# After the last U block, V blocks load into U's buffers, and the last LN weights and rows come later, from GpSimd's queue

## The chip, the cores and the metric

One core of a Trainium2 chip runs the whole program. The metric is the device time of one execution in microseconds, the median of several. Engines are named as in the profile: PE is TensorE, DVE VectorE, ACT ScalarE, POOL GpSimd, SP the engine that here only issues DMAs.

## The reference, cut to what matters

One layer of an encoder on 512 prompt frames and 32 sample frames of width 1024: a token mixer, a layer norm, then PEER (16384 single-neuron experts, 8 heads, the best 16 each) and a second layer norm. The change lies in PEER and the second norm:

```python
    t1, i1 = lax.top_k(s1, PEER_TOPK)
    t2, i2 = lax.top_k(s2, PEER_TOPK)
    ...
    g = jax.nn.softmax(top, axis=-1)
    u = jnp.take(u_tab, idx, axis=0)
    act = jax.nn.gelu(jnp.einsum("nhkd,nd->nhk", u, xb).astype(jnp.float32))
    vv = jnp.take(v_tab, idx, axis=0)
    return jnp.einsum("nhk,nhkd->nd", (g * act).astype(xb.dtype), vv)
...
    y = layer_norm(DN_ALPHA * h + peer_ffn(h, peer_w_query, peer_keys_1, peer_keys_2, peer_u, peer_v), ln2_g, ln2_b)
```

## The kernel before

The expert stage takes the last 1,000 us or so. 384 of the 544 tokens are done densely: all 16384 experts are computed for them in 128 blocks of 128 experts. Block b of the U table gives the activations `acts` (`up`), later these are multiplied with a matrix of gates that is zero where an expert was not chosen, and block b of the V table is multiplied with them and added up in six PSUM banks (`down`). The other tokens, the sample frames (`S`) and the last 128 prompt frames (`P3`), are done by gathers: an indirect DMA of GpSimd fetches one chosen row of U or V for each of 128 partitions into a tile `gat`, and VectorE makes a dot product of it (L1100) or adds it to `acc` (L1115).

Matmuls of 32-bit numbers are made of three products: every operand is split into a high part (a cast on ScalarE) and a low part (a subtraction on VectorE). For a block of V that is `vr`, the raw tile that SP loads, `vh` (L1184) and `vl` (L1185); for the gated activations `pwh` (L1217) and `pwl` (L1218). A block of V is 18 matmuls of 512 columns.

The loop of `experts` runs over `it`. In each step it computes U block `it`, and V block b = it - 27 (AHEAD is 27). From it = 128 on only V blocks are left, 101 to 127, of which the last four stand behind the loop. Each V block also loads `gt`, a piece of the gate matrix, into one of three buffers (L1204), multiplied into `acts` at L1211. A few gathers follow in each step; each waits for the load of that step's block (`pace`).

The tiles of one tag share a ring of buffers: 6 of tag `u` (raw, high and low part of U blocks), 8 of tag `v` (the same of V blocks), 6 of `gat` (gathered rows, the raw tiles of the last four V blocks, the scratch of the second layer norm), two of `pwh` and `pwl`. An instruction that fills a buffer waits for all who used it before. At it = 128 `ln_loads` puts the two weight rows `lnw` of the second layer norm into `u` buffers, at it = 132 `rows_back` puts the three 128-row tiles `hback` there that hold the dense tokens' residual. Both are issued from ScalarE's queue.

The order of each engine's instructions is not that of the code: a scheduler sorts them when the program is built. An engine then executes its own strictly in order, and a DMA that has to wait for its buffer holds up all that stands behind it on the same queue.

Of the kernel before, what the change touches and what calls it, by code (L numbers as in the profile page):

```python
# [32 lines left out]
P = 128  # L33
# [12 lines left out]
NK = 128  # L46
# [41 lines left out]
AHEAD = 27  # L88
# [5 lines left out]
NV = 8  # L94
GATHER = AHEAD
RATE = (1, 1), (28, 10), (31, 10), (12, 10)
BACK = 4
ROUTE = (5, 2), (1, 1)


class Build:
# [1044 lines left out]
    def experts(self, es):  # L1146
        tc, nc, A = self.tc, self.nc, self.A
# [28 lines left out]
        acts, ups, vload, gg = self.acts, {}, {}, {}  # L1176

        def table(ap, name, stage=None):
            tile_ = dict(gat=lambda dt, n: pool.tile([P, D], dt, tag="gat", name=n, bufs=NGAT), u=lambda dt, n: pool.tile([P, D], dt, tag="u", name=n, bufs=NU),
                         v=lambda dt, n: self.vtile(dt, [P, D], n))  # L1180
            raw = tile_[stage or name](F32, name + "r")
            h, l = (tile_[name](F32R, name + s) for s in "hl")
            load = nc.sync.dma_start(raw, ap)
            nc.scalar.copy(h, raw)  # L1184
            nc.vector.tensor_tensor(out=l, in0=raw, in1=h.bitcast(F32), op=OP.subtract)  # L1185
            return h, l, load

        def up(b):
            a = pool.tile([P, ND], F32, tag="acts", name="acts", bufs=NACT)
            uh, ul, load = table(A["u_chunk"][b], "u")  # L1190
            ps = ubank()[:, :ND]
            for k in range(KD):
                sl = slice(k * P, (k + 1) * P)
                _, mm = self.mm3(ps, uh[:, sl], ul[:, sl], self.hDh[:, k, TS:], self.hDl[:, k, TS:], k == 0, k == KD - 1)
            ups[b] = load, mm
            nc.scalar.activation(a, ps, GELU)  # L1196
            acts[b] = a

        def down(b):

            if not out:
                out.extend([ybank(i, half) for half in range(2)] for i in range(NDT))
            gt = pool.tile([P, NS], F32, tag="gt", name="gt", bufs=3)
            i = nc.sync.dma_start(gt, gates[b * P:(b + 1) * P])  # L1204

            load, mm = ups[min(b + AHEAD, NK - 1)]
            tc.add_manual_dep(i.ins, load.ins.name, ORDER, reason="queue order")
            for s in [i for c in self.scatters.values() for i in c]:
                tc.add_manual_dep(i.ins, s.ins.name, SYNC, reason="all heads are in")
            a = acts.pop(b)  # L1210
            nc.vector.tensor_tensor(out=a[:, :NS], in0=a[:, :NS], in1=gt, op=OP.mult)  # L1211
            a2 = a[:, NS:].rearrange("p (q t) -> p q t", t=GT)
            nc.vector.tensor_tensor(out=a2, in0=a2, in1=gg[b // GB][:, :, b % GB], op=OP.mult)
            last = b >= NK - LAST
            wh, wl = (pool.tile([P, ND], F32R, name="pw" + s, **(dict(tag="acts", bufs=NACT) if last else dict(tag="pw" + s, bufs=2)))
                      for s in "hl")
            nc.scalar.copy(wh, a)  # L1217
            nc.vector.tensor_tensor(out=wl, in0=a, in1=wh.bitcast(F32), op=OP.subtract)  # L1218
            vh, vl, vload[b] = table(A["peer_v"][b * P:(b + 1) * P], "v", "gat" if last else None)

            def products(i, halves=range(2)):
                ts = slice(i * P, (i + 1) * P)
                for half in halves:
                    cs = slice(half * 512, (half + 1) * 512)
                    first, _ = self.mm3(out[i][half], wh[:, ts], wl[:, ts], vh[:, cs], vl[:, cs], b == 0, b == NK - 1)
                    tc.add_manual_dep(first.ins, mm.ins.name, ORDER, reason="queue order")

            return products

        def gates_in(c):  # L1230

            g = gg[c] = pool.tile([P, (ND - NS) // GT, GB, GT], F32, tag="gg", name="gg", bufs=2)
            src = self.G2[:, :, c * GB * GT:(c + 1) * GB * GT].rearrange("q p x -> p q x")
            nc.sync.dma_start(g.rearrange("p q b t -> p q (b t)"), src)

        def ln_loads():

            self.lnw = [pool.tile([P, D], F32, tag="u", name="lnw", bufs=NU) for _ in range(2)]
            for w, row in zip(self.lnw, range(2, 4)):
                nc.scalar.dma_start(w, self.bcast(A["ln"][row]))  # L1240

        def rows_back():
            for t in dense:
                t.h = pool.tile([P, D], F32, tag="u", name="hback", bufs=NU)
                nc.scalar.dma_start(t.h, self.hS[t.dense:t.dense + t.n])

        def gather(n):
            for step in steps[:n]:
                step()
            del steps[:n]  # L1250

        for it in range(EARLY, NK + AHEAD - LAST):
            if it < NK:
                up(it)
            b = it - AHEAD
            if b >= -1 and (b + 1) % GB == 0 and b + 1 < NK:
                assert not build
                gates_in((b + 1) // GB)
            if b >= 0:
                p = down(b)  # L1260
                for i in range(NDT):
                    p(i)

            a, c = ROUTE[b >= 0]
            for _ in range((it + 1) * BUILD[0] // BUILD[1] - it * BUILD[0] // BUILD[1]):

                if build and (len(build) == 2 or not self.bg):
                    build[0].pop(0)()
                    if not build[0]:
                        del build[0]  # L1270
            if not build:
                for _ in range((it + 1) * a // c - it * a // c):
                    if self.late:
                        self.late.pop(0)()
            for _ in range((it + 1) * a // c - it * a // c):
                if self.bg:
                    self.bg.pop(0)()
            if it == NK:
                ln_loads()
            if it == NK + BACK:  # L1280
                rows_back()
            if it < GATHER:
                continue
            a, c = RATE[0 if b < 0 else 1 if self.late else 2 if it < NK else 3]
            self.pace = ups[it][0] if it < NK else vload[b]
            gather((it + 1) * a // c - it * a // c)
        gather(len(steps))
        ps = [down(b) for b in range(NK - LAST, NK)]
        for t in gathered:
            self.finish(t.n, t.h, t.stat2, A["o_ys"] if t.prompt is None else A["o_yp"][t.prompt:t.prompt + t.n], pool)  # L1290
# [84 lines left out]
```

## Time and profile before

| | |
|---|---|
| median of 3 runs | 1825.83 us (1819.69 to 1826.23) |
| the profiled execution | 1829.75 us |
| its span, first to last instruction | 1828.0 us |
| mean granted clock of TensorE | 0.970 |
| TensorE, VectorE, ScalarE, GpSimd busy | 93%, 77%, 46%, 50% |
| bytes moved | 442.98 MB |

The shares are means over the whole span; the stages differ, so the rows below are cut by time. A releaser is the work whose end let an instruction start. SPq and ACTq are the instructions with which SP and ScalarE issue DMAs; one that waits for a buffer is shown as long as it stands there.

### The profile page before, as it was taken

To read this page: it belongs to the slowest core of one execution; us is meant where nothing else is said; L and a number is where in the kernel's file an instruction comes from. 1 tells how busy PE (TensorE), PEld (TensorE's weight loads), DVE (VectorE), ACT (ScalarE), POOL (GpSimd) and SP (SyncE) were. 2 spreads that over 40 slices of the span, in tenths; PEclk is the share of its full clock that TensorE was granted. 3 is DMA by queue.
4 is the path that set the end of the run, shared out by engine and by line. 5 is a ranking of instruction groups with operands and counts; after the bars stand their busy time and mean duration, and the time that the engine had idled before them with its cause. 6 is when DMAs were issued, how large, how long until landed. Compare 5 with 4: busy or idle time off the path is not lost.

```text
span 1828.0 us, 27122 instructions
## 1 busy us (share of the span) xinstructions
PE 1701.5 (93%) x9579; PEld 1532.9 (84%) x9579; DVE 1404.5 (77%) x2935; ACT 848.6 (46%) x1516; POOL 919.6 (50%) x621
## 2 busy tenths in 40 slices
PE   8999989986988999949999999999999999999797
PEld 7779879975878999848899899999999899998576
DVE  6633777897686698638989888888888888887665
ACT  7644344785545597915436243333333333332232
POOL 2100233878888888874545745444444545563200
PEclk9999989997998999978999999999999999999999
DMA  9843635654565665659999899999999999998751
GB/s 318 282 136 104 197 104 162 151 137 84 94 170 129 152 163 121 177 142 329 332 327 345 320 355 340 353 329 344 345 354 336 348 330 335 345 335 287 233 203 47
DMA packets 189945, 442.98 MB, mean 242 GB/s; under 512 B 45496, under 2 KB 89192, under 8 KB 188272
## 3 DMA queue, kind: packets, MB, share of 16 engines
q1 hardware_dynamic: 109408, 265.76, 43.0%
q0 software_dynamic: 74752, 167.91, 29.2%
q10 hardware_dynamic: 5648, 7.58, 1.3%
q8 instruction: 75, 1.23, 0.3%
q14 instruction: 62, 0.51, 0.1%
HBM read 409.80 MB, written 31.33 MB: 241 GB/s over the span
## 4 chain that ended last, share of the span: by engine, by line
PE 66%; DMA 5%; DVE 5%; POOL 4%; ACT 4%; issue 2%; SPq 0%; DVEq 0%; POOLq 0%; ACTq 0%
PE y L163 9%; PE y L164 9%; PE y L160 9%; PE u L160 8%; PE u L163 8%; PE u L164 8%; POOL gatemat L1018 4%; PE mm L160 4%; PE mm L164 3%; PE mm L163 3%; DMA gat<-peer_v,idxP 1%; DMA gatemat<-gateP,idxP 1%; DMA ur<-u_chunk 1%; PE x L894 1%; PE x L586 1%
## 5 line engine op out<-in xcount | busy, mean ns | idle before, releaser
L1018 POOL DMA_INDIRECT gatemat<-gateP,idxP x256 | 422.9, 1652 | 121.3 <-issue 103.2
L160 PE MATMUL u<-hDh,uh 128*128 128x384 f32 x992 | 340.8, 344 | 30.0 <-ACT acts L1196 23.1
L164 PE MATMUL u<-hDh,ul 128*128 128x384 f32 x992 | 336.9, 340 | 1.6 <-DVE ul L1185 1.5
L163 PE MATMUL u<-hDl,uh 128*128 128x384 f32 x992 | 337.5, 340 | 0.0
L163 PE MATMUL y<-vl,pwh 128*128 128x512 f32 x768 | 301.9, 396 | 9.2 <-DVE vl L1185 9.2
L164 PE MATMUL y<-vh,pwl 128*128 128x512 f32 x768 | 299.7, 396 | 0.0
L160 PE MATMUL y<-vh,pwh 128*128 128x512 f32 x768 | 290.2, 396 | 8.1 <-ACT vh L1184 8.1
L1090 POOL DMA_INDIRECT gat<-peer_v,idxP x128 | 167.1, 1305 | 216.8 <-DVE accP L1115 46.5
L1090 POOL DMA_INDIRECT gat<-peer_u,idxP x128 | 184.3, 1440 | 168.2 <-DMA ur<-u_chunk 62.5
L118 DVE TENSOR_TENSOR wl<-raw,wh 128x1024 fp32r<-128x1024 f32 (+1 forms) x134 | 164.7, 1231 | 78.7 <-ACT wh L114 76.1
L160 PEld LDWEIGHTS u<-hDh,uh 128*128 128x128 f32 x992 | 188.2, 190 | 37.0 <-ACT acts L1196 23.8
L114 ACT CAST wh<-raw 128x1024 fp32r<-128x1024 f32 (+1 forms) x140 | 145.1, 1039 | 155.5 <-PE mm L163 119.1
L163 PEld LDWEIGHTS u<-hDl,uh 128*128 128x128 f32 x992 | 188.2, 190 | 4.3
L164 PEld LDWEIGHTS u<-hDh,ul 128*128 128x128 f32 x992 | 187.9, 189 | 3.2 <-DVE ul L1185 3.2
L1185 DVE TENSOR_TENSOR vl<-vr,vh 128x1024 fp32r<-128x1024 f32 x128 | 156.1, 1220 | 32.6 <-ACT vh L1184 31.1
L1217 ACT CAST pwh<-acts 128x384 fp32r<-128x384 f32 x128 | 65.3, 513 | 248.6 <-PE y L163 127.1
L163 PEld LDWEIGHTS y<-vl,pwh 128*128 128x128 f32 x768 | 145.5, 189 | 41.3 <-DVE vl L1185 11.8
L160 PEld LDWEIGHTS y<-vh,pwh 128*128 128x128 f32 x768 | 144.6, 189 | 39.8 <-ACT vh L1184 11.1
L1184 ACT CAST vh<-vr 128x1024 fp32r<-128x1024 f32 x128 | 133.9, 1047 | 90.0 <-DMA vr<-peer_v 66.7
L1185 DVE TENSOR_TENSOR ul<-ur,uh 128x1024 fp32r<-128x1024 f32 x124 | 151.2, 1220 | 31.6 <-ACT uh L1184 28.2
L1115 DVE SCALAR_TENSOR_TENSOR accP<-gat,actP,accP 128x1024 f32<-128x1024 f32 x127 | 162.9, 1283 | 15.4 <-DMA gat<-peer_v,idxP 14.8
L164 PEld LDWEIGHTS y<-vh,pwl 128*128 128x128 f32 x768 | 145.2, 189 | 33.8
(367 smaller groups left out, 3583.2 us busy)
## 6 DMA issues: line engine op xcount, KB each, us to landing
vr<-peer_v SPq DMA_DIRECT2D x128, 512.0 KB, 6.9
ur<-u_chunk SPq DMA_DIRECT2D x124, 512.0 KB, 5.0
raw<-w_chunk SPq DMA_DIRECT2D x63, 512.0 KB, 3.7
raw<-w_q SPq DMA_DIRECT2D x32, 512.0 KB, 3.5
gatemat<-zero SPq DMA_DIRECT2D x24, 512.0 KB, 6.3
gatemat<-stage SPq DMA_DIRECT2D x12, 1024.0 KB, 4.5
gg<-gatemat SPq DMA_DIRECT2D x16, 768.0 KB, 8.1
gt<-gatemat SPq DMA_DIRECT2D x128, 96.0 KB, 6.1
```

The costliest lines, as they stand in the source:

```text
L114: nc.scalar.copy(h, src)
L118: eng.tensor_tensor(out=l, in0=src, in1=h.bitcast(F32), op=OP.subtract)
L160: first = nc.tensor.matmul(out, lh, rh, start=start, stop=False)
L163: nc.tensor.matmul(out, lh, rl, start=False, stop=False)
L164: return first, nc.tensor.matmul(out, ll, rh, start=False, stop=stop)
L586: first = nc.tensor.matmul(ps[:n, :nk], self.qa[:, h, t.col:t.col + n], t.keys[:, h], start=True, stop=False)
L1018: i = nc.gpsimd.indirect_dma_start(out=self.G, out_offset=bass.IndirectOffsetOnAxis(ap=t.idx[:n, j:j + 1], axis=0), in_=t.gate[:n, j:j + 1 ...
L1090: i = nc.gpsimd.indirect_dma_start(out=r, out_offset=None, in_=A[table], in_offset=bass.IndirectOffsetOnAxis(ap=t.idx[:, j:j + 1], axis=0))
L1115: nc.vector.scalar_tensor_tensor(out=acc, in0=r, scalar=act[:, j:j + 1], in1=acc, op0=OP.mult, op1=OP.add)
L1184: nc.scalar.copy(h, raw)
L1185: nc.vector.tensor_tensor(out=l, in0=raw, in1=h.bitcast(F32), op=OP.subtract)
L1217: nc.scalar.copy(wh, a)
```

## The change

The raw tile of a V block goes into a `u` buffer for blocks 101 to 119 (`NK - AHEAD <= b < BACK`, with BACK now 120). Blocks 120 to 123 use `v` buffers as before, the last four `gat`. The weight rows and the `hback` tiles are loaded at block 120, when eight blocks are left, into the same `u` buffers, and their DMAs are issued from GpSimd's queue.

```diff
-BACK = 4
+BACK = 120
...
-            vh, vl, vload[b] = table(A["peer_v"][b * P:(b + 1) * P], "v", "gat" if last else None)
+            vh, vl, vload[b] = table(A["peer_v"][b * P:(b + 1) * P], "v", "gat" if last else "u" if NK - AHEAD <= b < BACK else None)
...
             for w, row in zip(self.lnw, range(2, 4)):
-                nc.scalar.dma_start(w, self.bcast(A["ln"][row]))
+                nc.gpsimd.dma_start(w, self.bcast(A["ln"][row]))
...
                 t.h = pool.tile([P, D], F32, tag="u", name="hback", bufs=NU)
-                nc.scalar.dma_start(t.h, self.hS[t.dense:t.dense + t.n])
+                nc.gpsimd.dma_start(t.h, self.hS[t.dense:t.dense + t.n])
...
-            if it == NK:
+            if b == BACK:
                 ln_loads()
-            if it == NK + BACK:
                 rows_back()
```

Up to the last U blocks every engine's order is the same as before. Behind that it differs. First SP's queue, from the `gt` load of block 101 to the V loads of blocks 103 and 106; `vr_16633` is block 101 in both, `vr_16672` and `vr_16712` are 102 and 103 of the kernel before. Before:

```order
L1204 DMA gt_16625<-gatemat_150 128x192
L1204 DMA gt_16664<-gatemat_150 128x192
L1183 DMA vr_16633<-peer_v 128x1024
L1204 DMA gt_16704<-gatemat_150 128x192
L1204 DMA gt_16739<-gatemat_150 128x192
L1204 DMA gt_16774<-gatemat_150 128x192
L1183 DMA vr_16672<-peer_v 128x1024
L1204 DMA gt_16815<-gatemat_150 128x192
L1204 DMA gt_16850<-gatemat_150 128x192
L1204 DMA gt_16888<-gatemat_150 128x192
L1204 DMA gt_16923<-gatemat_150 128x192
L1183 DMA vr_16712<-peer_v 128x1024
```

And after, where `vr_16633`, `vr_16668`, `vr_16708`, `vr_16743`, `vr_16778` and `vr_16813` are blocks 101 to 106:

```order
L1204 DMA gt_16625<-gatemat_150 128x192
L1204 DMA gt_16660<-gatemat_150 128x192
L1204 DMA gt_16700<-gatemat_150 128x192
L1183 DMA vr_16633<-peer_v 128x1024
L1183 DMA vr_16668<-peer_v 128x1024
L1183 DMA vr_16708<-peer_v 128x1024
L1183 DMA vr_16743<-peer_v 128x1024
L1204 DMA gt_16735<-gatemat_150 128x192
L1204 DMA gt_16770<-gatemat_150 128x192
L1204 DMA gt_16805<-gatemat_150 128x192
L1183 DMA vr_16778<-peer_v 128x1024
L1183 DMA vr_16813<-peer_v 128x1024
```

The V loads of four blocks now stand together; before, three or four `gt` loads stood between any two. The load of block 101 has moved behind one `gt` load more. The order of the `gt` loads of later blocks has moved back: before, all of them stood ahead of the V load of block 108; after, those of the last twelve blocks stand behind the V load of block 119.

Second, VectorE where it computes the second layer norm of the gathered tokens (`y_17475` those of S, `y_17495` those of P3) between the splits of two V blocks. Before, between those of blocks 112 and 113:

```order
L1185 TENSOR_TENSOR vl_17040<-vr_17038,vh_17039 128x1024
L1142 SCALAR_TENSOR_TENSOR y_17475<-y_17475,stat2S_10786,lnw_16658 32x512 x2
L1139 SCALAR_TENSOR_TENSOR y_17495<-hP3_6238,stat2P3_17062,lnw_16657 128x1024
L697 TENSOR_SCALAR stat2P3_17062<-stat2P3_17062 128x1
L1185 TENSOR_TENSOR vl_17075<-vr_17073,vh_17074 128x1024
```

After, between those of blocks 117 and 118 (the `acts` rows are the gate products of blocks 116 and 117):

```order
L1185 TENSOR_TENSOR vl_17193<-vr_17191,vh_17192 128x1024
L1218 TENSOR_TENSOR pwl_17124<-acts_15654,pwh_17123 128x384
L1139 SCALAR_TENSOR_TENSOR y_17475<-hS_2381,stat2S_10786,lnw_17313 32x1024
L1139 SCALAR_TENSOR_TENSOR y_17495<-hP3_6238,stat2P3_17052,lnw_17313 128x1024
L697 TENSOR_SCALAR stat2P3_17052<-stat2P3_17052 128x1
L1211 TENSOR_TENSOR acts_15728<-acts_15728,gt_17151 128x192
L1142 SCALAR_TENSOR_TENSOR y_17475<-y_17475,stat2S_10786,lnw_17314 32x512 x2
L1211 TENSOR_TENSOR acts_15804<-acts_15804,gt_17183 128x192
L1185 TENSOR_TENSOR vl_17225<-vr_17223,vh_17224 128x1024
```

The layer norm of S and P3 has moved back by five blocks, and the gate products, which before all stood ahead of it, now stand between its steps. Behind these rows come the other steps of P3's layer norm, mixed with the gate products of blocks 118 to 127. SP's two output DMAs of P3 stand ahead of the V loads of blocks 121 and 122; before, they stood ahead of that of block 116.

Third, ScalarE in the last blocks before the four behind the loop. Before, from block 119 (`vh_17268`) to block 122; `vh` and `pwh` of the same block follow each other:

```order
L1184 CAST vh_17268<-vr_17267 128x1024
L1217 CAST pwh_17263<-acts_15952 128x384
L1184 CAST vh_17300<-vr_17299 128x1024
L1217 CAST pwh_17295<-acts_16029 128x384
L1184 CAST vh_17332<-vr_17331 128x1024
L1217 CAST pwh_17327<-acts_16103 128x384
L1184 CAST vh_17364<-vr_17363 128x1024
L1217 CAST pwh_17359<-acts_16177 128x384
```

After, from `pwh` of block 119 to that of 122; `vh_17332` is block 121:

```order
L1217 CAST pwh_17253<-acts_15952 128x384
L1184 CAST vh_17332<-vr_17331 128x1024
L1217 CAST pwh_17285<-acts_16029 128x384
L1184 CAST vh_17364<-vr_17363 128x1024
L1217 CAST pwh_17327<-acts_16103 128x384
L1184 CAST vh_17396<-vr_17395 128x1024
L1217 CAST pwh_17359<-acts_16177 128x384
```

Here `pwh` of a block stands behind `vh` of the block after it. On GpSimd the five moved loads stand behind the last gather, at the end of its program.

## Rows read from the trace of the kernel before

**Rows 1.** The page's part 2: 40 slices of the span, busy tenths.

```profile
PE   8999989986988999949999999999999999999797
...
DMA  9843635654565665659999899999999999998751
GB/s 318 282 136 104 197 104 162 151 137 84 94 170 129 152 163 121 177 142 329 332 327 345 320 355 340 353 329 344 345 354 336 348 330 335 345 335 287 233 203 47
```

**Rows 2.** Busy time by stretch: length, then PE, PEld, DVE, ACT, POOL; clock; DMA.

```profile
1000.00:1676.80 676.80, 675.65 (x3378) 610.92 (x3377) 570.97 (x797) 234.45 (x328) 341.67 (x245) 1.00 0.93 339
1676.80:1760.00 83.20, 65.95 (x259) 49.41 (x258) 57.15 (x102) 24.28 (x36) 13.33 (x12) 0.96 0.67 223
1760.00:1817.30 57.30, 57.30 (x248) 46.31 (x246) 29.90 (x58) 19.29 (x26) 0.00 (x0) 1.00 0.23 78
```

**Rows 3.** Timeline of PE: one V block's bounds, V100's first and the last matmul.

```profile
1559.25 0.39 PE L160 MATMUL y<-vh,pwh 128*128 128x512 f32 x1
...
1563.42 0.34 PE L160 MATMUL u<-hDh,uh 128*128 128x384 f32 x1
...
1676.76 0.39 PE L160 MATMUL y<-vh,pwh 128*128 128x512 f32 x1
...
1817.13 0.39 PE L164 MATMUL y<-vh,pwl 128*128 128x512 f32 x1
```

**Rows 4.** Waits of PE, 1676 to 1760: total us, times, longest.

```profile
PE y L163 <- DVE vl L1185: 9.2, 6, 2.8
PE y L160 <- ACT vh L1184: 8.1, 7, 1.5
```

**Rows 5.** The same columns as rows 2, for 6 us.

```profile
1728.00:1734.00 6.00, 5.75 (x14) 4.49 (x15) 4.39 (x6) 0.66 (x2) 1.22 (x1) 0.50 0.44 140
```

**Rows 6.** Timeline of SP's queue: start us, length us, what it issues.

```profile
1656.86 0.38 SPq L1183 DMA_DIRECT2D vr<-peer_v  x1
1664.83 3.98 SPq L1204 DMA_DIRECT2D gt<-gatemat  x3
1668.92 0.53 SPq L1183 DMA_DIRECT2D vr<-peer_v  x1
1673.99 14.05 SPq L1204 DMA_DIRECT2D gt<-gatemat  x4
1688.10 0.42 SPq L1183 DMA_DIRECT2D vr<-peer_v  x1
```

**Rows 7.** Waits of SP's queue, 1676 to 1760.

```profile
SPq L1204 <- DVE acts L1211: 25.2, 13, 7.6
...
SPq L1183 <- PE y L164: 10.0, 4, 3.5
...
SPq L1183 <- PE y L163: 5.1, 1, 5.1
```

**Rows 8.** V loads issued 1680 to 1740, then 1740 to 1800: issue to landing.

```profile
DMA to landing us min/median/max: 7.7/7.7/7.7
...
DMA to landing us min/median/max: 3.2/3.2/3.2
```

**Rows 9.** DVE, 1676 to 1760, groups by shape: busy us, mean ns; idle before.

```profile
L1185 DVE TENSOR_TENSOR vl<-vr,vh 128x1024 fp32r<-128x1024 f32 x13 | 15.8, 1219 | 2.4 <-ACT vh L1184 2.4
...
L1211 DVE TENSOR_TENSOR acts<-acts,gt 128x192 f32<-128x192 f32 x24 | 7.9, 352 | 3.1 <-DMA gt<-gatemat 3.1
...
L704 DVE SCALAR_TENSOR_TENSOR stat2S<-stat2S 32x1 f32<-32x1 f32 x3 | 0.6, 203 | 0.1
```

**Rows 10.** ACT, the same view and stretch.

```profile
L1184 ACT CAST vh<-vr 128x1024 fp32r<-128x1024 f32 x14 | 14.6, 1045 | 21.6 <-DMA vr<-peer_v 20.7 <-DVE vl L1185 0.9
L1217 ACT CAST pwh<-acts 128x384 fp32r<-128x384 f32 x17 | 8.4, 510 | 34.8 <-PE y L163 28.1 <-DVE acts L1211 6.6
```

**Rows 11.** Loads of `gt` issued 1600 to 1680, then 1680 to 1718: issue to landing.

```profile
DMA to landing us min/median/max: 6.7/6.7/6.7
...
DMA to landing us min/median/max: 1.8/2.2/2.9
```

**Rows 12.** The weight rows' loads: issue (ns min/median/max), then issue to landing.

```profile
L1240 ACTq DMA_DIRECT2D lnw<-ln x2: 346/346/346, 1665.0 to 1668.6; - x2
...
DMA to landing us min/median/max: 7.5/7.5/7.5
```

**Rows 13.** Gathers from V, 1640 to 1760: POOL's ns min/median/max; to landing.

```profile
L1090 POOL DMA_INDIRECT gat<-peer_v,idxP x16: 932/946/1948, 1658.4 to 1739.3; - x16
...
DMA to landing us min/median/max: 4.2/5.7/7.7
```

## The prediction

> **What bounds the kernel now.** I read the page's 40 slices first. From the 19th slice on TensorE is at 9 and the DMA engines at 8 or 9; then the DMA engines fall to 8, 7 and 5 in slices 37 to 39, the bytes from 335 to 287, 233 and 203 GB/s, and TensorE drops to 7 in slice 38 [rows 1]. So I cut the end into three stretches by time. From 1000 to 1676.8 us TensorE is busy for 675.65 of 676.80 us: U and V blocks alternate and nothing is to be had there without fewer matmuls. From 1676.8, where the last U matmul is issued, to 1760 it is busy for only 65.95 of 83.20 us, with the DMA engines at 0.67. From 1760 on it is full again [rows 2].
>
> How much is there to win? One V block (18 matmuls) takes 1563.42 - 1559.25 = 4.17 us where nothing waits. The 28 blocks V100 to V127 run from 1676.76 to 1817.13 + 0.39 = 1817.52, that is 140.8 us [rows 3]; 28 x 4.17 is 116.8, and the last matmul's modelled end adds 0.2. **The ceiling is therefore 23.8 us**, all of it before 1760. Of it 17.3 us are waits by name: 9.2 for VectorE's `vl` and 8.1 for ScalarE's `vh`, in 13 pieces [rows 4]. Between 1728 and 1734, after a wait of 2.8 us, the granted clock was 0.50, the 1.2 GHz level [rows 5]; some twelve matmuls went at double spacing, 12 x 0.195 = 2.3 us. The remaining 4.2 us are the 13 restarts, 0.3 each.
>
> Who is late behind `vh` and `vl`? The loads. On SP's queue the load of V101 is issued at 1656.86, of V102 at 1668.92, and that of V103 only at 1688.10: between the last two the queue stood for 14 us in four `gt` loads [rows 6]. SP's waits in this stretch are for the product that frees a `gt` buffer (25.2 us) and for the matmuls that free a V buffer (10.0 and 5.1) [rows 7]. With raw, high and low part of a block in 8 V buffers, the load of block b can start only when block b-3 has been multiplied: two blocks, 8.3 us, have to cover the load, the cast and the subtraction. A load lands in 7.7 us here and in 3.2 us after 1740 [rows 8]; cast and subtraction are 1.05 and 1.22 us [rows 9, 10]. 7.7 + 2.3 is more than 8.3, 3.2 + 2.3 is less: this is why TensorE waits before 1760 and not after.
>
> **The change, part by part.** *Raw V tiles of blocks 101 to 119 in U's buffers.* In the built order V102 and V103 wait for the matmuls of U126, V104 for U127's split, V105 for U127's matmuls. U126 ends two blocks ahead of V100, at about 1676.8 - 8.4 = 1668.4, so V102 is issued there as before, but V103 and V104 go out right behind it instead of at 1688 and later. Landing 7.7 us later and split in 2.3, V102 is ready at 1678.4, and V102's turn is 1685.1. From V107 on a load needs only the split of the block six earlier; `vh` and `vl` have the 8 V buffers for themselves and need the matmuls of the block four earlier. Cast and subtraction run three blocks, 12.5 us, ahead of need. The 17.3 us of waits, the slow clock behind them and their restarts go.
>
> *V101's load moves back.* It now stands behind the third `gt` load, whose group in the queue started at 1664.83 [rows 6], so about 1665.2 instead of 1656.86. Landed by 1672.9 and split by 1675.2, it has 5.7 us to V101's start at 1680.9. Cost zero; past 5.7 us it would cost one for one.
>
> *Can VectorE and the DMA engines follow?* VectorE's work of the stretch, 57.15 us [rows 2], has to fit in 83.2 - 18.6 = 64.6 us: 88% busy, where the U and V stage ran at 571/677 = 84% with no wait of TensorE. The bytes, 223 GB/s x 83.2 us = 18.6 MB, come at 288 GB/s; the stage before sustained 339. It fits, but VectorE with little air, and it executes in order. I follow it block by block with the durations of [rows 9, 10]. At V113 it is tight: `pwh` of 113 waits for a `gt` product that stands behind the split of 115 (released by V111's end) and eight small layer-norm steps. V111's end + cast 1.05 + subtraction 1.22 + small steps 1.4 + product 0.35 + cast 0.51 = 4.5 us, against the 4.17 of V112. I book 0.3 us of wait for each of V113 to V118, 1.8 us.
>
> *The last blocks.* V120 to V123 load into V buffers again. V122's raw tile takes a buffer that V119's matmuls free, and ScalarE's order now has `vh` of V122 ahead of `pwh` of V121, which V121's first matmul needs (before, `vh` and `pwh` of the same block stood together). So V121 starts at V119's end + landing + 1.05 + 0.51 + 0.2 of handovers. With 3.2 us to land that is 0.8 us later than V120's 4.17, with 7.7 it is 5.3. I take 3.7 us and **1.3 us**, near the light end, since after 1740 little is left to load. V122 and V123 follow at the same distance and lose nothing more. The seven waits booked so far bring 7 restarts, 2.1 us.
>
> *`gt` loads bunched at the end.* In the built order the products with `gt` of V116 to V127 come close together on VectorE, with three `gt` buffers, and `pwl` of V118 stands behind V124's. A `gt` load landed in 6.7 us in the full stage and in 2.2 us (at most 2.9) between 1680 and 1718 [rows 11]. With 2.9 us three rounds of loads end by 1751, and V118 needs its `pwl` at about 1753.5: nothing lost. With 6.7 us each round is late by some 4.5 us; V118, V119 and V120 would lose about 5.7, 4.8 and 3.5. I take the row of the lighter stretch: zero.
>
> *LN weights and rows from GpSimd's queue.* ScalarE loses five issues of some 0.35 us; it is busy 24.28 of 83.2 us, so nothing is won. Behind the last gather nothing is queued on GpSimd. The first weight row waits for the split of V114 (about 1725.7), the second for V115's (1729.3). On ScalarE's queue such a row took 7.5 us to land [rows 12]; the gathers, the only transfers of this queue here, took GpSimd 0.9 to 1.9 us and landed in 4.2 to 7.7 us [rows 13]. So they are there by 1735.3 and 1738.9. VectorE first wants them behind V117's split, at 1738.6 and 1741.5: no wait. The rows of h come later still and are needed only behind the last matmul. What stands behind the last matmul keeps its order: 1828.0 - 1817.5 = 10.5 us as before.
>
> A rule of the Trainium skill (SBUF - State Buffer, section "SBUF: two separate sides") speaks against this move: a DMA issued from GpSimd has its descriptors written by GpSimd's cores, which VectorE can lock out of a shared port, and the page advises the other queues. The spread of 0.9 to 1.9 us on GpSimd [rows 13] may be that, but no row here tells it apart. By the row the sum stays as it is; by the rule without a bound it is the last rival below.
>
> **Sum.** 23.8 - 1.8 - 1.3 - 2.1 = 18.6 us.
>
> **Rivals.** (1) *The knot at the end*: `gt` and V loads land late once the loads bunch, up to 5.7 + 4.8 + 3.5 + 5.3 = 19 us of new waits, a gain of 4 to 15 us, 1811 to 1822. For it: [rows 11] has a 6.7; against it: that was at full DMA load. (2) *VectorE or the DMA engines become the bound from V101 on*: 0.5 us lost in each of 20 blocks, a gain of 4 to 12, 1814 to 1822. For it: 88%; against: 84% went without a wait. (3) *The waits only move*, because SP's queue still stands behind `gt` loads: gain near zero, 1826. Against it: four V loads in a row stand in the new order. (4) *Slower, by the LN weights*: VectorE meets the layer-norm step that reads the second weight row ahead of V118's split, and SP holds V121 to V123 behind the output DMA of that layer norm. There are about 2 us of slack; from then on every us that the weights land late moves the end. To undo the gain and lose 9 more they must land near 1771, 42 us after their issue, against 7.5 on the other queue; 1835 then.
>
> **Numbers.** The profiled execution took 1829.75 us (span 1828.0); less 18.6 it is 1811.2. The median of the runs is 1825.83, so I predict **1807 us**. Forecast 64% (gain 15 to 23.8: 1802 to 1811), rival 1 18%, rival 2 10%, rival 3 4%, rival 4 4%. 0.5% is 9.1 us, about what a measurement can tell from no change. Half of rivals 1 and 2 lies above that: faster 0.78, same 0.18, slower 0.04. The range goes from 1800 (the ceiling and 2 us of scatter between runs) to 1820, which leaves out rivals 3 and 4 and the worst of 1 and 2.
>
> **What the profile after should show.** Between the last U matmul and 1740 the waits of TensorE for `vh` and `vl` fall from 17.3 us to under 3; V102 to V104 are issued within 2 us of each other; the clock stays at 1.00; one wait of 1 to 2 us for `pwh` at V121; GpSimd issues the weights after its last gather and nobody waits for them. It is wrong if VectorE is late for `pwl` throughout (rival 2), if SP's `gt` waits still come right ahead of late V loads (rival 3), or if a layer-norm step or an output DMA is named as the releaser (rival 4).

## The result and the profile after

The changed kernel takes 1804.67 us (median of 5 runs, 1802.68 to 1808.34), the kernel before 1825.83 (5 runs, 1819.69 to 1828.33). The ratio is 0.9888, with a 95% interval of 0.9872 to 0.9905: 21 us or 1.1% faster.

The slices of the page, as in [rows 1]:

```profile
PE   8999989985998999966999999999999999999997
...
DMA  8843635654555665567989899999999999998961
GB/s 322 282 143 106 199 106 153 153 129 95 95 145 136 153 164 141 164 176 251 344 313 364 316 332 354 349 341 331 357 342 351 335 335 346 338 343 310 360 208 47
```

TensorE's dip in slice 38 is gone. In the same slices the DMA engines moved 310, 360 and 208 GB/s, where 287, 233 and 203 stood before. The windows, with the columns of [rows 2], and TensorE's bounds, as in [rows 3]:

```profile
1674.86:1760.00 85.14, 85.14 (x368) 69.03 (x368) 69.33 (x117) 35.11 (x50) 18.08 (x16) 1.00 0.78 273
1676.80:1720.00 43.20, 43.20 (x188) 35.02 (x187) 37.38 (x46) 16.84 (x24) 14.03 (x9) 1.00 0.98 367
1760.00:1792.20 32.20, 32.13 (x139) 25.72 (x137) 17.22 (x43) 8.46 (x11) 0.00 (x0) 1.00 0.04 17
```

```profile
1674.68 0.34 PE L164 MATMUL u<-hDh,ul 128*128 128x384 f32 x1
1674.86 0.39 PE L160 MATMUL y<-vh,pwh 128*128 128x512 f32 x1
...
1791.74 0.39 PE L164 MATMUL y<-vh,pwl 128*128 128x512 f32 x1
```

TensorE is busy for the whole of the V-only stretch, at full clock, and the list of its waits, from 1600 us to the end, is empty: the 17.3 us of [rows 4] and the slow clock of [rows 5] are gone. From the last U matmul to the last matmul it takes 1791.74 - 1674.68 = 117.06 us, against 140.55 before (1676.58 to 1817.13). This distance is used below for every kernel, because the stages ahead of it scatter: over the eleven profiles the last U matmul comes at 1667.0 to 1680.4 us. Of the 25.1 us between the two profiled executions, 1.9 are such scatter, 23.5 come out of this stretch, and what stands behind the last matmul takes 0.3 more.

SP's queue, as in [rows 6]:

```profile
1649.21 14.04 SPq L1204 DMA_DIRECT2D gt<-gatemat  x4
1663.35 4.42 SPq L1183 DMA_DIRECT2D vr<-peer_v  x4
1667.86 1.83 SPq L1204 DMA_DIRECT2D gt<-gatemat  x3
1674.87 4.42 SPq L1183 DMA_DIRECT2D vr<-peer_v  x5
```

V101 to V104 stand together and go out within 4.4 us, V105 to V109 behind three short `gt` loads. V104 is wanted only at 1674.86 + 4 x 4.18 = 1691.6, so its load has some 24 us. SP still stands behind `gt` loads, 24.7 us in the stretch where [rows 7] had 25.2, but the V loads that TensorE needs next are out by then.

### The profile page after: what moved, and what is told of

The parts are those of the page before. It is cut to its first block, busy times and chain, and to the rows that moved or that the text cites. A ratio compares the mean times of both kernels' runs of the same rounds, so it can differ in the third digit from the quotient of the medians.

```text
span 1802.9 us, 27133 instructions
## 1 busy us (share of the span) xinstructions
PE 1691.9 (94%) x9579; PEld 1529.1 (85%) x9579; DVE 1404.2 (78%) x2935; ACT 847.7 (47%) x1516; POOL 922.8 (51%) x626
## 4 chain that ended last, share of the span: by engine, by line
PE 66%; POOL 7%; DVE 6%; issue 2%; ACT 2%; DMA 2%; SPq 0%; DVEq 0%; POOLq 0%; ACTq 0%
PE y L164 10%; PE y L160 10%; PE y L163 10%; PE u L160 8%; PE u L163 8%; PE u L164 8%; POOL gatemat L1018 7%; PE mm L160 3%; PE mm L164 3%; PE mm L163 3%; DMA gatemat<-gateP,idxP 1%; DVE wl L118 1%; PE x L894 1%; DVE hot L1054 1%; PE x L586 1%
## 5 line engine op out<-in xcount | busy, mean ns | idle before, releaser
L160 PE MATMUL y<-vh,pwh 128*128 128x512 f32 x768 | 302.7, 394 | 0.0
L164 PE MATMUL y<-vh,pwl 128*128 128x512 f32 x768 | 289.9, 394 | 0.0
L1090 POOL DMA_INDIRECT gat<-peer_v,idxP x128 | 175.4, 1370 | 180.4 <-DMA ur<-u_chunk 57.4
L1090 POOL DMA_INDIRECT gat<-peer_u,idxP x128 | 180.5, 1410 | 170.2 <-DMA ur<-u_chunk 60.5
```

The costliest lines, as they stand in the source:

```text
L160: first = nc.tensor.matmul(out, lh, rh, start=start, stop=False)
L164: return first, nc.tensor.matmul(out, ll, rh, start=False, stop=stop)
L1090: i = nc.gpsimd.indirect_dma_start(out=r, out_offset=None, in_=A[table], in_offset=bass.IndirectOffsetOnAxis(ap=t.idx[:, j:j + 1], axis=0))
```

## The experiments

Theory at the start, from the prediction: the V loads are late, because 8 V buffers give a load two blocks of time and because SP's queue stands in `gt` loads; U's buffers cure that. Rivals: it was the early 2.6 MB of weights and rows, or ScalarE's queue; or the queue's order alone. The table sums up; "stretch" is from the last U matmul to the last matmul of the profiled execution, "waits" are TensorE's by name in it. Every ratio is against runs of before on the same chip (medians 1825.83 for the change, 1825.49 for the next four rows, 1827.95 for the three after them, 1823.79 for the last two). It is worked out from all runs, so it can differ by 0.1% from the quotient of the two medians. The stretch and the waits come from one profile for each kernel, and the runs of one kernel spread over up to 12 us.

| kernel | median us | ratio to before (95%) | stretch us | waits us |
|---|---|---|---|---|
| before | 1825.83 | | 140.55 | 17.3 |
| change | 1804.67 | 0.9888 (0.9872 to 0.9905) | 117.06 | 0 |
| weights from ScalarE | 1801.97 | 0.9862 (0.9839 to 0.9885) | 117.06 | 0 |
| weights and rows only | 1825.96 | 1.0000 (0.9984 to 1.0015) | 136.56 | 14.0 |
| before, `gt` behind V | 1814.26 | 0.9934 (0.9912 to 0.9956) | 131.38 | 10.0 |
| change, 104 for 120 | 1825.91 | 0.9999 (0.9985 to 1.0013) | 139.14 | 18.2 |
| before, V in order | 1810.79 | 0.9918 (0.9892 to 0.9944) | 119.96 | 2.0 |
| change, 110 for 120 | 1822.01 | 0.9977 (0.9961 to 0.9994) | 130.26 | 10.1 |
| change, 123 for 120 | 1805.10 | 0.9891 (0.9866 to 0.9916) | 117.06 | 0 |
| change again | 1803.40 | 0.9883 (0.9863 to 0.9903) | 117.06 | 0 |
| weights from ScalarE again | 1803.24 | 0.9887 (0.9870 to 0.9903) | 117.06 | 0 |

**The two halves apart.** The change with its five late loads on ScalarE's queue, and the five late loads alone (each edit is against the change):

```diff
-                nc.gpsimd.dma_start(w, self.bcast(A["ln"][row]))
+                nc.scalar.dma_start(w, self.bcast(A["ln"][row]))
...
-                nc.gpsimd.dma_start(t.h, self.hS[t.dense:t.dense + t.n])
+                nc.scalar.dma_start(t.h, self.hS[t.dense:t.dense + t.n])
```

> The change as it is, but the two weight rows and the three hback tiles are issued from ScalarE's queue again, still at block 120 and behind the V tiles in U's buffers. Theory (the U buffers alone give the gain; the queue of the five moved loads is neutral): ratio to before 0.988 to 0.990, about 1805 to 1808 us; TensorE's waits for vh and vl after the last U matmul stay under 1 us. ScalarE loses five issues of 0.35 us and stands up to 1 us in each for its buffer, with pwh of 113 to 116 behind it, so 0 to 2 us of waits for pwh are possible. Rival A (GpSimd's queue was needed, since a weight load that waits on ScalarE's queue holds up the casts): 5 us or more are lost, 1810 or above. Rival B (loads issued from GpSimd are slow or in VectorE's way): this kernel is faster than the change, 1800 to 1803, and the weights land sooner than there.

```diff
-            vh, vl, vload[b] = table(A["peer_v"][b * P:(b + 1) * P], "v", "gat" if last else "u" if NK - AHEAD <= b < BACK else None)
+            vh, vl, vload[b] = table(A["peer_v"][b * P:(b + 1) * P], "v", "gat" if last else None)
```

> Only the second half of the change: weight rows and hback are issued at block 120 in the code and from GpSimd's queue; the raw V tiles stay in the V buffers. Theory: the V loads are as late as before, so TensorE's waits for vh and vl after the last U matmul stay at 15 to 20 us and the time within 0.3% of before, 1820 to 1831 us. Rival (the 2.6 MB of weights and rows, or ScalarE's queue, made the V loads late): most of the gain is here already, 1805 to 1812 us, waits under 6 us.

The whole gain sits in the raw V tiles in U's buffers: without that half the time is that of before, with 14.0 us of waits, a little under the 15 to 20 expected. The queue of the weights was less clear, since ScalarE's came out 2.7 us lower in another set of runs, at 1801.97 us and inside the range of rival B. So both were run side by side:

> The change once more, beside the next kernel on the same chip, to tell the two queues of the moved loads apart. In the profiles both had 117.06 us from the last U matmul to the last matmul. Theory (GpSimd's and ScalarE's queue are the same here): the two medians within 2 us of each other, both 0.986 to 0.990 of before; 117.1 us again in that stretch. Rival (loads issued from GpSimd cost something): this one 3 us or more above the next.

> The change with weights and rows issued from ScalarE, once more. Theory: as the change, within 2 us; 117.1 us from the last U matmul to the last matmul. Rival: 3 us or more faster than the change, with the difference behind the last U matmul.

1803.40 and 1803.24 us: no difference. Of the 5.8 us between the two profiled spans (1800.7 and 1794.9), 5.55 lie ahead of the last U matmul (1672.57 and 1667.02). Rival A and rival B fall.

**Queue or buffers?** The kernel before, with one order added:

```diff
             tc.add_manual_dep(i.ins, load.ins.name, ORDER, reason="queue order")
+            if b + AHEAD >= NK:
+                tc.add_manual_dep(i.ins, vload[b - 1].ins.name, ORDER, reason="queue order")
```

> The kernel before with one order added: from block 101 on the gt load of block b stands behind the V load of block b-1 on SP's queue, so that no V load stands behind a gt load of a later block. V buffers as before. Theory (two blocks of cover, 8.3 us, are less than 7.7 us of landing and 2.3 of split): SP's V loads wait for TensorE instead of gt, one wait of about 1.7 us remains in every third block while loads take 7.7 us; 5 to 9 us of waits for vh and vl remain of 17.3, the time is 1813 to 1821 us. Rival (the gt loads ahead in the queue are the whole cause, the V buffers none): waits under 3 us and 1803 to 1809 us, as the change. Second rival (the gt loads only cover for the V buffers): no gain, 15 us or more of waits.

More than half of the gain by the ratio, without a buffer more; in the profile, which is of the slowest of its six runs (1820.06 us), 9.2 of the 23.5 us. The sum looked like the first theory, the place of the waits did not. From 1676.8 to 1715 there was none, where before 9.2 of the 17.3 us of [rows 4] lay; then came three (windows, then TensorE's timeline, with the wait and its releaser in brackets):

```profile
1676.80:1715.00 38.20, 38.20 (x166) 30.87 (x165) 27.31 (x34) 12.43 (x17) 8.63 (x8) 1.00 0.78 253
```

```profile
1717.06 0.50 PE L163 MATMUL y<-vl,pwh 128*128 128x512 f32 x1 [1.41 <-DVE vl L1185]
1727.38 0.79 PE L163 MATMUL y<-vl,pwh 128*128 128x512 f32 x1 [5.87 <-DVE vl L1185]
1740.41 0.50 PE L163 MATMUL y<-vl,pwh 128*128 128x512 f32 x1 [2.68 <-DVE stat2S L710]
```

In this kernel's queue the loads of the last four blocks, which go into `gat` and wait for gathers, stood ahead of V loads needed sooner. The next kernel takes that away too; its output DMAs come behind the last V load.

```diff
             vh, vl, vload[b] = table(A["peer_v"][b * P:(b + 1) * P], "v", "gat" if last else None)
+            if b + AHEAD >= NK:
+                tc.add_manual_dep(vload[b].ins, vload[b - 1].ins.name, ORDER, reason="queue order")
```

> The kernel before with two orders added for blocks 101 to 127: the gt load of block b behind the V load of block b-1, and the V load of block b behind that of b-1 (so that no load into gat stands ahead of earlier blocks). SP's queue is then one gt, one V load, one gt, in order of blocks; all output DMAs stand behind the last V load; V buffers, weights and rows as before. Theory (what was late was SP's queue; two blocks of cover in 8 V buffers are enough once loads land in under 5 us, as five of the six of V104 to V109 did in the run with gt behind V): waits of TensorE under 3 us, 1802 to 1809 us, the gain of the change without U's buffers. Rival (the buffers are the second half of the cause, with 7.7 us of landing and 2.3 of split against 8.3): 5 to 9 us of waits, 1811 to 1818 us, and the loads' landings above 6 us where the waits are.

One wait is left, and it is not for a load: at 1710.92 TensorE waited 2.0 us for `vl`, and VectorE's split stood behind an `accP` step that waited 3.31 us for a gather:

```profile
1708.18 1.28 DVE L1115 SCALAR_TENSOR_TENSOR accP<-gat,actP,accP 128x1024 f32<-128x1024 f32 x1 [3.31 <-DMA gat<-peer_v,idxP]
1709.39 0.35 DVE L1213 TENSOR_TENSOR acts<-acts,gt 128x192 f32<-128x192 f32 x1
1709.65 1.22 DVE L1185 TENSOR_TENSOR vl<-vr,vh 128x1024 fp32r<-128x1024 f32 x1
```

So 20.6 of the 23.5 us come back with two orders asked for on SP's queue: the number of V buffers was not what bound. By the medians it is 17.2 (1827.95 to 1810.79); the waits are as the theory had them, the time lies between the two ranges. 1.4 us of the difference between 20.6 and 17.2 lie behind the last matmul, 12.3 us to the end instead of 10.9. The layer norm of the gathered tokens runs later here, its output DMAs go out at 1789 instead of 1758, but that is still ahead of the last matmul (1797.73), and whether it makes the 1.4 us is not shown. The other 2 us are not explained; they are no more than the runs scatter.

The edit asks for order on SP's queue alone, but the scheduler sorted ScalarE's instructions anew as well. In this kernel `vh` of V102 follows `pwh` of V102:

```profile
1682.09 0.51 ACT L1219 CAST pwh<-acts 128x384 fp32r<-128x384 f32 x1 [3.20 <-PE y L163]
1682.51 1.05 ACT L1184 CAST vh<-vr 128x1024 fp32r<-128x1024 f32 x1
```

Before, it stood behind `pwh` of V103 and started one block later. So the run tells order from buffers, but not SP's order from ScalarE's; no run changes one of them alone.

**How many blocks?** 104, 110 and 123 in the place of 120:

```diff
-BACK = 120
+BACK = 104
```

> The change with 104 in the place of 120: only the raw tiles of V101 to V103 go into U's buffers, weights and rows come behind them. Theory (the gain goes with the blocks that have early loads): the waits of the first blocks go, those of V106 to V115 stay, since SP's queue from the fifth V load on is ordered as before; 8 to 14 us of waits remain, gain 3 to 8 us, 1817 to 1823 us. Rival (a head start of a few blocks is kept to the end): waits under 4 us, 1804 to 1810 us.

> The change with 110 in the place of 120: V101 to V109 into U's buffers, weights and rows behind them, V110 and later into V buffers, with one V load between groups of gt loads on SP's queue from the tenth V load on. 104 gave no gain at all with waits as before from V105 on. Theory (every V load behind a gt group is late, whatever was gained earlier): TensorE has no wait up to V109; behind it 4 to 10 us of waits, in groups that follow SP's gt waits; 1808 to 1816 us. Rival (once the last gathers are over, near V107, loads land in 3 to 5 us and the V buffers do): waits under 3 us, 1803 to 1808 us.

> The change with 123 in the place of 120: V101 to V122 into U's buffers; the weights wait for splits three blocks later, so they are issued some 12 us later, near 1736 and 1739 us. Theory (TensorE has no wait left in the change, and the layer norm of the gathered tokens has room): the same time as the change within 0.3%, 0.987 to 0.990 of before; no wait of TensorE. Rival (the later weights hold VectorE at the layer norm of the gathered tokens, with splits behind it): waits of TensorE for vl or pwl of 3 to 10 us near V118 to V121, 1808 to 1816 us.

The gain does not go with the number of blocks. With 104 it is nothing, against both theories: from the fourth V load on, one V load again stands between groups of three or four `gt` loads, and 18.2 us of waits remain. With 110 it is a fifth by the ratio and 10.3 of the 23.5 us by the stretch, with 120 and 123 all. In the kernel with 110, the V blocks with early loads run full (1680.5 to 1721.5), then TensorE falls to 33.34 of 43.5 us. First two windows, then SP's queue, then ScalarE:

```profile
1680.50:1721.50 41.00, 41.00 (x179) 33.26 (x178) 32.19 (x40) 12.70 (x18) 12.89 (x14) 1.00 0.83 298
1721.50:1765.00 43.50, 33.34 (x132) 24.78 (x131) 30.29 (x69) 15.60 (x24) 0.94 (x1) 0.96 0.63 200
```

```profile
1709.76 0.33 SPq L1183 DMA_DIRECT2D vr<-peer_v  x1
1716.54 7.53 SPq L1204 DMA_DIRECT2D gt<-gatemat  x4
1724.18 0.38 SPq L1183 DMA_DIRECT2D vr<-peer_v  x1
```

```profile
1722.35 0.51 ACT L1217 CAST pwh<-acts 128x384 fp32r<-128x384 f32 x1 [3.66 <-PE y L163]
1722.77 1.04 ACT L1184 CAST vh<-vr 128x1024 fp32r<-128x1024 f32 x1
1728.52 1.04 ACT L1184 CAST vh<-vr 128x1024 fp32r<-128x1024 f32 x1 [4.71 <-DMA vr<-peer_v]
```

Two delays are seen here. The load issued at 1724.18 stood behind four `gt` loads, and its cast at 1728.52 waited for it. The cast at 1722.77 had its load long before (1709.76), but stands on ScalarE behind a `pwh` that waited 3.66 us for TensorE. The head start of nine blocks is then used up within two. The theory had the place right and the size too small: 10.1 us of waits, some 3 more for half clock and restarts (13.2 in the stretch), and 1822 us, above the 1808 to 1816 expected. With 123 the weights go out at 1735.6 and 1739.8; VectorE waits 0.3 us for one of them, TensorE for nothing.

## Why the prediction was right

The forecast was 1807 us, a gain of 18.6; measured is 1804.67 and 21.2. The number came from two things that held: the ceiling, and the built order, from which the times of the loads were read. Of the two causes that the prediction names for the waits, the `gt` loads on SP's queue held and the two blocks of time in 8 V buffers did not, as the step at the end of this section shows. That the medians lie only 2.6 us from the forecast is in part luck: in the stretch itself 23.5 us came where 18.6 were forecast.

**The ceiling.** 23.8 us were read as what the stretch could give at most; 23.5 came. That part of the sum was right.

**The terms that were taken off.** 5.2 us of new waits were booked, and none is there. (a) 1.8 us for V113 to V118, from a chain that begins at V111's end. The cast of V115 began at 1723.86, 1.2 us before that end (1725.05): TensorE's order puts the six products with `pwl` last in V111, and the buffer that the cast takes was free when the last product with `vl` was done. `pwh` of V113 was there at 1728.83, V113 began at 1729.23:

```profile
1723.86 1.05 ACT L1184 CAST vh<-vr 128x1024 fp32r<-128x1024 f32 x1 [2.67 <-PE y L163]
1728.32 0.51 ACT L1217 CAST pwh<-acts 128x384 fp32r<-128x384 f32 x1 [3.42 <-DVE acts L1211]
```

```profile
1723.66 1.56 PE L164 MATMUL y<-vh,pwl 128*128 128x512 f32 x6
1725.05 0.40 PE L160 MATMUL y<-vh,pwh 128*128 128x512 f32 x1
...
1729.23 0.39 PE L160 MATMUL y<-vh,pwh 128*128 128x512 f32 x1
```

So the chain was tight as booked at V113, with 0.4 us to spare instead of 0.3 lacking. (b) 1.3 us for V121. V122's raw tile did not have to wait for V119: its load went out at 1754.57, at V118's end, a block earlier than I had it. `vh` of 122 and `pwh` of 121, in the order foreseen, were done by 1759.73, and V121 began at 1762.70:

```profile
1754.57 4.50 SPq L1183 DMA_DIRECT2D vr<-peer_v  x2
```

```profile
1758.26 1.05 ACT L1184 CAST vh<-vr 128x1024 fp32r<-128x1024 f32 x1 [1.28 <-DMA vr<-peer_v]
1759.22 0.51 ACT L1217 CAST pwh<-acts 128x384 fp32r<-128x384 f32 x1
```

```profile
1762.70 0.39 PE L160 MATMUL y<-vh,pwh 128*128 128x512 f32 x1
```

(c) The 2.1 us of restarts go with the waits.

**The terms at zero** held. V101's later load, at 1663.35, held up nobody. The one `gt` load behind 1718 whose landing the profile has took 2.8 us, and VectorE waited for such loads three times, 2.5 us in all, TensorE not. VectorE was busy 37.38 of 43.20 us up to 1720, 87% and so near the 88% feared, and 81% over the 85.14 us; TensorE did not wait for it. The weights were issued at 1723.77 and 1726.83, their first reader on VectorE started at 1735.28 without a wait. A DMA issued from GpSimd took longer to issue than from ScalarE, as the next rows show, the change first and then the kernel with ScalarE's queue, but with the same time in the end:

```profile
L1240 POOL DMA_DIRECT2D lnw<-ln x2: 555/566/577, 1723.8 to 1726.8; - x2
```

```profile
L1240 ACTq DMA_DIRECT2D lnw<-ln x2: 346/346/346, 1721.8 to 1724.5; - x2
```

The rule of the Trainium skill that spoke against this queue (SBUF - State Buffer, section "SBUF: two separate sides") may hold, but it costs nothing here: there are 11 us from the issue of a weight row to its first reader, the two `hback` loads with a landing in the profile took 3.6 and 4.1 us, and the two queues gave 1803.40 and 1803.24 us.

**The step that was wrong** is the sentence on cause, "7.7 + 2.3 is more than 8.3 ... this is why TensorE waits". The 7.7 us of [rows 8] are one load of the 14 in that window: minimum, median and maximum are the same number. It is the load issued at 1735.01, the last of four that went out within 1.7 us, and I took it for all. Two issues of SP's queue and then ScalarE's timeline, both of the kernel before, tell another:

```profile
1688.10 0.42 SPq L1183 DMA_DIRECT2D vr<-peer_v  x1
...
1699.87 0.54 SPq L1183 DMA_DIRECT2D vr<-peer_v  x1
```

```profile
1685.13 0.51 ACT L1217 CAST pwh<-acts 128x384 fp32r<-128x384 f32 x1 [3.72 <-PE y L163]
1685.55 1.04 ACT L1184 CAST vh<-vr 128x1024 fp32r<-128x1024 f32 x1
1691.89 1.04 ACT L1184 CAST vh<-vr 128x1024 fp32r<-128x1024 f32 x1 [5.30 <-DMA vr<-peer_v]
...
1704.45 1.04 ACT L1184 CAST vh<-vr 128x1024 fp32r<-128x1024 f32 x1 [5.76 <-DMA vr<-peer_v]
```

V103's load went out at 1688.10 and its cast, which waited for it, began 3.8 us later; V105's took 4.6. With 2.3 us of split that is less than the 8.3 of two blocks. V103's load was late because SP stood in `gt` loads until 1688.0, 7 us past V100's end (1680.9), from which the prediction has its buffer free. Even that bound is not fixed: with V in order, V103's load went out at 1673.59, before V100 began (1677.94), so the two blocks of the prediction do not bound every load.

```profile
1673.59 0.33 SPq L1183 DMA_DIRECT2D vr<-peer_v  x1
```

The kernel with V in order bears it out: it has no buffer more and loses only 2.9 us against the change in the stretch. V106's load there went out at 1694.63 and its cast began at 1701.48, 6.9 us later, and TensorE did not wait. V102's cast at 1685.55 shows a second delay that the prediction did not name: it stands behind a `pwh` that waited for TensorE, and TensorE then waited 1.4 us for it. V104's cast (1697.65) and V112's (1746.87) stand the same way, with waits of 1.3 and 1.4 us: these three make 4.0 of the 17.3 us, and the waits for `vl` right behind them 3.9 more. So the change seems to work by where the scheduler puts the loads and casts when early buffers are there: four and five V loads in a row, casts ahead of `pwh`. U's buffers with the old order, which would show it, were not run. The kernel with 110 shows what happens when that order ends. Whether two blocks would be too little with loads as slow as the 10.2 us of the last section was not tried.

## What to carry to other kernels

When a load is late, compare its issue with the moment its buffer came free: a difference is the queue's order, not the number of buffers, and a reordering that needs no memory may give most of what more buffers give. An order that is added on one queue can move the instructions of other engines too; look at them before the gain is put down to that queue. A duration whose minimum, median and maximum are equal is one sample, and one whose median is the mean of the other two can be two; before a sum rests on it, look for others, such as the distance from an issue to a cast that waited for it. When the last stage alone is changed, measure that stage from its first to its last instruction, since the stages ahead of it can scatter by more than the effect.

## What was not expected of the hardware

V loads landed slowly in the first part of the stretch after the change, and TensorE did not notice. This is the row for the loads issued from 1676 to 1700:

```profile
DMA to landing us min/median/max: 6.3/8.2/10.2
```

Only two of the eight loads have a landing in the profile, 10.2 us for the one issued at 1677.83 and 6.3 for that at 1694.30; the 8.2 is their mean. Before, V103's and V105's casts began 3.8 and 4.6 us after the issue. The DMA engines were busy at 0.98 and moved 367 GB/s from 1676.8 to 1720, more than the 339 of the U and V stage [rows 2]; the lead of the loads hid it.

TensorE's clock did not follow the length of the wait alone. After waits of 2.8 us (before, [rows 5]), 5.9 (`gt` behind V) and 3.9 (110) the matmuls behind them showed the 1.2 GHz level, with a granted clock of 0.50, 0.50 and 0.57 in the few us that follow. In the kernel with 104 it was 0.50 behind a wait of 2.4 us that ended at 1699.25, and 1.00 behind one of 3.4 that ended at 1717.52:

```profile
1699.00:1702.00 3.00, 2.75 (x7) 2.17 (x8) 2.31 (x6) 1.05 (x1) 0.34 (x1) 0.50 0.60 211
1717.00:1721.00 4.00, 3.48 (x15) 2.87 (x16) 3.59 (x7) 0.92 (x3) 0.94 (x1) 1.00 0.69 182
```

What decides it stays open.
